# Where tiles begin in SBUF: small tiles first, matmul operands at multiples of 512 bytes

## The chip, the core and the metric

The kernel runs on one NeuronCore of a Trainium2 chip as one launch. The metric is the device time of that launch in microseconds, the median of three runs. Besides it there is one profiled execution, from which all rows below are taken; its span runs from the first to the last instruction of the program and doesn't contain what lies around them.

## What is computed

A trunk of two layers over 256 tokens of width 1024, everything in float32:

```python
for i in range(DEPTH):                       # DEPTH = 2
    y = gmlp_mixer(x, ...) if i == 0 else mlstm_mixer(x, ...)
    x = layer_norm(ALPHA * x + y, ln1_g[i], ln1_b[i])
    x = layer_norm(ALPHA * x + swiglu(x, ffn_w_gate[i], ffn_w_up[i], ffn_w_down[i]),
                   ln2_g[i], ln2_b[i])
    gate = jax.nn.sigmoid(x @ ple_w_gate[i] + ple_b_gate[i])
    x = x + gate * (p[i] @ ple_w_proj[i])
```

The gMLP mixer is two products of width 3072 with a gating over positions between them. The mLSTM mixer is an input product, a short convolution, block-diagonal q, k and v, a causal matrix of 256 x 256 for each of four heads, and an output product. SwiGLU has 2816 hidden features.

## The kernel before

Every weight is read once, as blocks of 128 x 1024 float32 (512 KB), loaded ahead by the SP queue into slots named `raw`. ScalarE and VectorE split each block into two float32r parts, high and low, whose sum is the block (`split`, L136); they lie side by side in one tile `w` of 8192 bytes for each partition. Activations are split in the same way. Each product is made of three matmuls, high*high, high*low and low*high.

There are two kinds of products. In `mm_feat` (L195 to L197) a piece of 128 x 128 of the weight block is the stationary operand and 256 tokens of x (`xh`, `xl`) are the moving one. In `mm_tok` (L190 to L192) and `mm_part` (L216 to L219) 128 tokens (of `xh` and `xl`, or of the hidden features `h`) are the stationary operand, and 512 columns of the weight block move. Every matmul has a weight load of its own: 5367 of each.

The order of the work is that of the program text. TensorE goes through gMLP (`vps`, then `ups`, `svps` and the first `acc`), SwiGLU of layer 0 (`first`, `pg` and `pu`, `acc`), the embedding's gate (`gate`), mLSTM (`zf`, `xmps`, `zps`, `qps`, `gates`, `s`, `num`, `acc`) and SwiGLU and gate of layer 1. Transposes are called `tp`.

All tiles of SBUF come from one pool `sb`. A tile without a tag keeps its place for the whole program. A tile with a tag goes through a number of slots of the size of the largest tile of the tag (`BUFS`, L126). Places are given out in the order in which the text first asks for a tile or a tag, each rounded up to 32 bytes. At the bottom of every partition the program reserves a scratch area in which descriptors of dynamic DMAs would be generated, 16384 bytes by default; four constants follow in 128 bytes, then the pool.

With the sizes added up in that order, the tiles that matmuls read begin in the kernel before at these places, given as the remainder of the byte address by 512:

| tiles | remainder |
|---|---|
| `xh`, `xl`, `xn`, and all slots of `s`, `m2`, `raw` and `w` | 160 |
| slots of `b8` (the weight blocks in `WIDE`, `ws`, `vn`, `bdm`, `pt`, ...) and of `row` (`xm`) | 448 |
| slots of `h` (hidden features, `q`, some `xm`, `phi`, `plo`) | 224 |
| `ident`, `ones_r` | 128 |
| `wx` | 256 |

`xh` and `xl` are at 160 because `ident` (512 bytes) and `mhalf` (8 bytes, in 32) lie ahead of them behind 16384 + 128 bytes. Pieces of a tile that a matmul reads begin at multiples of 512 bytes from the tile's start, those of `wx` at multiples of 64. The last tile ends 224 bytes below the top of the partition.

Of the kernel before, what the change touches and what calls it, by code (L numbers as in the profile page):

```python
# [14 lines left out]
P = 128  # L15
D = 1024
S = 256
# [27 lines left out]
# Weight blocks that are kept while token tile 1 is still in a norm; they have  # L45
# slots of their own, and some are loaded earlier than their place in the order of use.
# [6 lines left out]
def down_blocks(f):  # L53
    """the feature blocks that go down after block f is made"""
    return range(4) if f == 3 + LAG else [f - LAG] if f > 3 + LAG else []


def weight_plan(a):
    """The weight blocks in the order in which they are used."""
    plan = []  # L60

    def add(key, ap):
        plan.append((key, ap))

    for c in range(6):
        for kp in range(4):
            add(("v", c, kp), a["gm_v"][c, kp])
    add(("u", 0), a["gm_u"][0])
    add(("u", 1), a["gm_u"][1])
    for s in range(NU + LAG_S):  # L70
        if s + 2 < NU:
            add(("u", s + 2), a["gm_u"][s + 2])
        if s >= LAG_S:
            add(("wo", s - LAG_S), a["gm_wo"][s - LAG_S])

    def ffn(l):
        add(("pj", l, 0), a["ple_proj"][l, 0])
        for n in ("g", "u"):
            for kp in range(4):
                add((n, l, kp), a["ffn_" + n][l, kp])  # L80
        for f in range(4, NF + LAG):
            for n in ("g", "u") if f < NF else ():
                add((n, l, f), a["ffn_" + n][l, f])
            for e in down_blocks(f):
                add(("d", l, e), a["ffn_d"][l, e])
        add(("pj", l, 1), a["ple_proj"][l, 1])
        for k in range(KD):
            add(("pg", l, k), a["ple_gate"][l, k])

    ffn(0)  # L90
    for kp in range(4):
        add(("z", kp), a["ml_z"][kp])
    for s in range(NI + 2):
        if s < NI:
            add(("xm", s), a["ml_xm"][s])
        if s >= 2 and s % 4 == 2:
            add(("bdv", s // 4), a["ml_bdv"][s // 4])
        if s in Z_AFTER_XM:
            add(("z", Z_AFTER_XM[s]), a["ml_z"][Z_AFTER_XM[s]])
    for f in range(8, NI):  # L100
        add(("z", f), a["ml_z"][f])
    for f in range(NI):
        add(("mo", f), a["ml_wo"][f])
    ffn(1)
    by_key = dict(plan)
    moved = set(EARLY.values())
    order = []
    for key, _ in plan:
        if key not in moved:
            order.append(key)  # L110
        if key in EARLY:
            order.append(EARLY[key])
    return [(key, by_key[key]) for key in order]
# [3 lines left out]
def trunk(ctx, tc, a, out):  # L117
# [7 lines left out]
    # Slots of SBUF by size, shared by all phases.  # L125
# [8 lines left out]
    def split(hi, lo, src, fast=False, sub=dve):  # L134
        """float32r parts whose sum is src"""
        return dve.tensor_copy(hi, src) if fast else act.copy(hi, src), sub.tensor_tensor(lo, src, hi.bitcast(F32), ALU.subtract)  # L136

    # ---- weights: blocks [128, n <= 1024], loaded ahead and split (index 0
    # the high parts, index 1 the low) ----
# [4 lines left out]
    def issue_after(ops):  # L144
        """what is emitted in this context comes behind ops on their engines"""
        stack = ExitStack()
        for op in ops:
            stack.enter_context(tc.issue_after(op.ins))
        return stack
# [32 lines left out]
    ident = sb.tile([P, P], F32, name="ident")  # L182
    mhalf = sb.tile([P, 2], F32, name="mhalf")
# [15 lines left out]
    def feat_from_x(ps, w):  # L199
        """ps[128 features, 256 tokens] = (x w)^T"""  # L200
        for k in range(KD):
            mm_feat(ps, w, slice(k * P, (k + 1) * P), xh[:, k, :], xl[:, k, :], k == 0, k == KD - 1)

    def tok_from_x(ps, t, ws, before=(None, None)):
        """ps[128 tokens of tile t, 512] = x w; ws: 4 blocks of two k each.
        before: a step of the low part and what to emit before it"""
        for i in range(2):
            for k in range(KD):
                if i == 1 and k == before[0]:
                    before[1]()  # L210
                mm_part(ps, i, t, k, ws[k // 2], HALF[k % 2])

    def mm_part(ps, i, t, k, w, c):
        """the products with the high (i = 0) or low part of x"""
        if i == 0:
            pe.matmul(ps, xh[:, k, TOK[t]], w[:, 0, c], start=k == 0, stop=False)  # L216
            pe.matmul(ps, xh[:, k, TOK[t]], w[:, 1, c], start=False, stop=False)
        else:
            pe.matmul(ps, xl[:, k, TOK[t]], w[:, 0, c], start=False, stop=k == KD - 1)  # L219

    class Down:
        """y[tok, 1024] summed over n blocks of features; token tile 1 of the
        last HOLD blocks comes after all of token tile 0."""
# [58 lines left out]
    # ================= layer 0: gated MLP over positions =================  # L282
# [23 lines left out]
    vst = sb.tile([P, 2, 6, 6], F32, name="vst")  # L306
    vs = []
    for c in range(6):
        if c == 4:
# [8 lines left out]
            gmp = sb.tile([P, NU, 2], F32, name="gmp")  # L318
            sp.dma_start(gmp, a["gm_gb"])
            ones_r = sb.tile([P, P], F32R, name="ones_r")  # L320
            ones = sb.tile([P, 2], F32, name="ones")
            cmask = sb.tile([P, P], F32, name="cmask")
# [3 lines left out]
            # R[g, t] = sum_s ws[g, t, s], the same in all partitions  # L326
# [24 lines left out]
    vmv = sb.tile([P, 2, 2], F32, name="vmv")  # L351
    vrs = sb.tile([P, 2], F32, name="vrs")
# [7 lines left out]
    def norm_v(c, t):  # L360
        """(v - mean) / deviation; the gain and the offset come with sv"""
        if t == 0:
            vns[c] = tl("b8", [P, 2, 2, 512], F32R, "vn")
        v, o = vns[c], vs[c][:, t, :]
        dve.tensor_scalar(o, o, vmv[:, t, 0:1], vrs[:, t:t + 1], ALU.subtract, ALU.mult)
        split(v[:, 0, t, :], v[:, 1, t, :], o)
# [10 lines left out]
    def sv_block(f):  # L377
# [6 lines left out]
        # gain (ws n) + (offset R + b_s)  # L384
# [20 lines left out]
    def load_p(l):  # L405
        """p^T in parts, kept over the channel mixer"""
        pr = tl("m2", [P, 2, S], name="pr")
        sp.dma_start(pr, a["pT"][l])
        pts[l] = tl("b8", [P, 2, 2, S], F32R, "pt")
        split(pts[l][:, 0], pts[l][:, 1], pr)  # L410
# [16 lines left out]
    # ================= SwiGLU, norms, per-layer embedding =================  # L427
    def channel_mixer(l, acc, last, hook=None):
# [20 lines left out]
        # The first 512 features by token tile, so that token tile 0 runs  # L449
        # while token tile 1 is still in the norm.  # L450
# [96 lines left out]
    # ================= layer 1: mLSTM =================  # L547
    selIF = sb.tile([16, 2, 4], F32, name="selIF")
    wx = sb.tile([P, 2 * NI, 16], F32R, name="wx")
    par = sb.tile([P, NI, 7], F32, name="par")  # L550
    gbias = sb.tile([4, 2], F32, name="gbias")
    bmask = sb.tile([P, 32, 4], F32, name="bmask")
    wm = sb.tile([P, 2, NI, 4], F32R, name="wm")

    def mlstm_prepare():
# [18 lines left out]
        def products(terms, width):  # L574
            """sum of c[tile, b] g[tile, :, b] over b and the terms"""
# [14 lines left out]
        # S = q k^T = xc (Wq Wk^T) xc^T, so that k need not be made  # L590
        s = products([(0, load("wk4", a["ml_wk4"], 4))], 4)
        split(wm[:, 0], wm[:, 1], s)
        # The gates' weights carried through the blocks of q, k and v:
        # gates = xm (Wv Gv) + xc (Wq Gq + Wk Gk)
# [4 lines left out]
    def mlstm(embed1):  # L599
# [15 lines left out]
        # the block diagonals Wq Wk^T of 8 blocks of 128 channels each  # L615
# [86 lines left out]
        def s_block(f):  # L702
            """S^T[s, t] = q_t . k_s for s <= t in blocks of 128"""
# [29 lines left out]
        # ---- gates: a = i - B, G_t = max(0, max_{s<=t} a_s), B = cumsum(log f);  # L733
        # P^T[s, t] = S^T * scale * exp(a_s - G_t) ----
# [7 lines left out]
        cols = sb.tile([P, 4, 4], F32, name="cols")  # L742
        ph = []
        gs = tl("s", [16, S], name="gs")
        with tc.manual_schedule(engines={mybir.EngineType.Activation}):
# [23 lines left out]
            # exp(-m), kept finite  # L769
# [26 lines left out]
        def pv_block(h):  # L796
# [15 lines left out]
            # h = num / max(|den|, exp(-m)), then its norm over the head  # L812
# [56 lines left out]
def lay_out(inputs):  # L869
    """Rearranges the inputs so that each block of weights is one transfer  # L870
    with 4 KB in a row for each partition."""
# [4 lines left out]
    def feat(w):  # L876
        """[1024, n*128] -> [n, 128 (k in block), 8 (block of k) * 128]"""
        return w.reshape(KD, P, -1, P).transpose(2, 1, 0, 3).reshape(-1, P, D)

    def tok(w):  # L880
        """[1024, n*512] -> [n, 4 (pairs of blocks of k), 128, 2 * 512]"""
        return w.reshape(4, 2, P, -1, 512).transpose(3, 0, 2, 1, 4).reshape(-1, 4, P, D)

    def mixed(w):
        """the first 512 columns as tok, the others as feat"""
        return np.concatenate([tok(w[:, :512])[0], feat(w[:, 512:])])

    def diag(w):
        """[512, 4, 4] -> block diagonals [16, 128, 128]"""
# [6 lines left out]
    def part(w):  # L896
        """[2048, ...] -> [128, 16, ...]"""
# [26 lines left out]
    def over_block(w):  # L924
        """[512 blocks, 4 (b), n] -> [128, 16, n, 4 (b)], each block's rows for all its 4 channels"""
# [31 lines left out]
```

## Time and profile before

| | |
|---|---|
| median of three runs | 857.32 us (856.63 to 857.6) |
| span of the profiled execution | 855.1 us |
| TensorE busy | 846.4 us, 5367 matmuls |
| VectorE busy | 580.4 us |
| ScalarE busy | 452.7 us |
| granted TensorE clock | 0.999 of full over the span |
| moved by DMA | 155.62 MB, 182 GB/s |

Matmuls are pipelined, and the duration that the trace gives to one overlaps that of the next. What a matmul takes from the time of the kernel is therefore read as a spacing, the time from its start to the start of the next one. In the timeline this is the difference of two rows' first columns. In the chain of waits a run of equal matmuls stands in one row with its count, and time by count is the spacing.

### The profile page before, as it was taken

Reading aid. Unit: us, or ns where it says so; the run is one execution under the profiler, and the core shown is the slowest. Engines: PE = TensorE matmul, PEld = TensorE weight load, DVE = VectorE, ACT = ScalarE, POOL = GpSimd, SP = SyncE. Lnnn points to the kernel's source line nnn. Section 1 sums busy time; section 2 is a strip of 40 time slices with the busy share of each in tenths; the row PEclk is TensorE's granted clock in tenths of the full one; section 3 lists DMA queues with packets and bytes.
Section 4 is the critical chain, followed back from the end, with each engine's and each line's share of the span. In section 5 each row is a group of like instructions: output and inputs, shape, how many; then the busy total and the mean of one; then the engine's idle time right before and its main releaser. Section 6 shows DMA issues by size and latency. Waiting matters only on the chain.

```text
span 855.1 us, 13770 instructions
## 1 busy us (share of the span) xinstructions
PE 846.4 (99%) x5367; PEld 759.1 (89%) x5367; DVE 580.4 (68%) x831; ACT 452.7 (53%) x722; POOL 154.9 (18%) x197
## 2 busy tenths in 40 slices
PE   8999999999999999999999999999999999999997
PEld 5889999998888999999889999897888899999986
DVE  6667985667854546466878877689884545476574
ACT  6565655455444444365347777777643444455422
POOL 1021653443100001500102333133310000000010
PEclk9999999999999999999999999999999999999999
DMA  8885465557375555568234444263655655577501
GB/s 294 287 300 169 149 212 180 171 203 243 140 247 181 194 176 192 178 229 279 82 111 161 136 136 144 73 222 124 239 162 184 197 176 195 176 243 249 194 2 50
DMA packets 44714, 155.62 MB, mean 182 GB/s; under 512 B 5224, under 2 KB 5992, under 8 KB 44648
## 3 DMA queue, kind: packets, MB, share of 16 engines
q1 hardware_dynamic: 44360, 154.47, 53.7%
q8 instruction: 42, 0.69, 0.3%
q10 hardware_dynamic: 288, 0.26, 0.1%
q14 instruction: 24, 0.20, 0.1%
HBM read 153.67 MB, written 1.05 MB: 181 GB/s over the span
## 4 chain that ended last, share of the span: by engine, by line
PE 93%; DVE 3%; DMA 1%; ACT 1%; POOL 0%; issue 0%; SPq 0%; DVEq 0%; ACTq 0%; POOLq 0%
PE acc L190 9%; PE acc L192 9%; PE acc L191 9%; PE pu L196 4%; PE pu L195 4%; PE pu L197 4%; PE pg L197 4%; PE pg L195 4%; PE pg L196 4%; PE ups L197 3%; PE ups L195 3%; PE ups L196 3%; PE vps L192 2%; PE vps L191 2%; PE vps L190 2%; PE xmps L195 2%
## 5 line engine op out<-in xcount | busy, mean ns | idle before, releaser
L136 DVE TENSOR_TENSOR w<-raw,w 128x1024 fp32r<-128x1024 f32 (+1 forms) x277 | 334.5, 1219 | 169.3 <-ACT w L136 168.0
L136 ACT CAST w<-raw 128x1024 fp32r<-128x1024 f32 (+1 forms) x276 | 284.9, 1040 | 199.2 <-issue 57.0
L190 PE MATMUL acc<-w,h 128*128 128x512 f32 x336 | 133.5, 397 | 0.8 <-ACT hn L830 0.8
L191 PE MATMUL acc<-w,h 128*128 128x512 f32 x336 | 132.8, 395 | 0.3 <-DVE h L136 0.3
L192 PE MATMUL acc<-w,h 128*128 128x512 f32 x336 | 132.8, 395 | 0.0
L195 PE MATMUL pu<-xh,w 128*128 128x256 f32 x288 | 81.5, 283 | 0.0
L196 PE MATMUL pu<-xl,w 128*128 128x256 f32 x288 | 81.5, 283 | 0.0
L195 PE MATMUL pg<-xh,w 128*128 128x256 f32 x288 | 81.5, 283 | 0.0
L197 PE MATMUL pu<-xh,w 128*128 128x256 f32 x288 | 81.4, 283 | 0.0
L197 PE MATMUL pg<-xh,w 128*128 128x256 f32 x288 | 81.3, 282 | 0.0
L196 PE MATMUL pg<-xl,w 128*128 128x256 f32 x288 | 81.1, 282 | 0.0
L192 PEld LDWEIGHTS acc<-w,h 128*128 128x128 f32 x336 | 63.2, 188 | 15.5
L190 PEld LDWEIGHTS acc<-w,h 128*128 128x128 f32 x336 | 63.4, 189 | 13.9 <-ACT hn L830 1.3
L191 PEld LDWEIGHTS acc<-w,h 128*128 128x128 f32 x336 | 63.2, 188 | 13.0 <-DVE h L136 0.7
L248 POOL TENSOR_SCALAR ve<-mv 128x1 f32<-128x1 f32 x8 | 6.2, 776 | 276.8 <-DVE mv L268 276.8
L196 PEld LDWEIGHTS pg<-xl,w 128*128 128x128 f32 x288 | 54.9, 191 | 1.5
L195 PEld LDWEIGHTS pg<-xh,w 128*128 128x128 f32 x288 | 54.9, 191 | 1.4
L195 PEld LDWEIGHTS pu<-xh,w 128*128 128x128 f32 x288 | 55.3, 192 | 0.0
L196 PEld LDWEIGHTS pu<-xl,w 128*128 128x128 f32 x288 | 55.3, 192 | 0.0
L197 PEld LDWEIGHTS pu<-xh,w 128*128 128x128 f32 x288 | 55.3, 192 | 0.0
L197 PEld LDWEIGHTS pg<-xh,w 128*128 128x128 f32 x288 | 54.9, 191 | 0.0
L197 PE MATMUL ups<-xh,w 128*128 128x256 f32 x192 | 54.2, 282 | 0.0
(237 smaller groups left out, 1803.3 us busy)
## 6 DMA issues: line engine op xcount, KB each, us to landing
raw<-in_ffn_g SPq DMA_DIRECT2D x44, 512.0 KB, 3.5
raw<-in_ffn_u SPq DMA_DIRECT2D x44, 512.0 KB, 3.5
raw<-in_ffn_d SPq DMA_DIRECT2D x44, 512.0 KB, 3.6
raw<-in_gm_u SPq DMA_DIRECT2D x24, 512.0 KB, 3.5
raw<-in_gm_wo SPq DMA_DIRECT2D x24, 512.0 KB, 3.5
raw<-in_gm_v SPq DMA_DIRECT2D x23, 512.0 KB, 5.5
raw<-in_ple_gate SPq DMA_DIRECT2D x16, 512.0 KB, 4.5
raw<-in_ml_z SPq DMA_DIRECT2D x16, 512.0 KB, 3.5
```

Of the source, the lines that this page charges most:

```text
L136: return dve.tensor_copy(hi, src) if fast else act.copy(hi, src), sub.tensor_tensor(lo, src, hi.bitcast(F32), ALU.subtract)
L190: pe.matmul(ps, lh, w[:, 0, c], start=start, stop=False)
L191: pe.matmul(ps, ll, w[:, 0, c], start=False, stop=False)
L192: pe.matmul(ps, lh, w[:, 1, c], start=False, stop=stop)
L195: pe.matmul(ps, w[:, 0, c], h, start=start, stop=False)
L196: pe.matmul(ps, w[:, 0, c], l, start=False, stop=False)
L197: pe.matmul(ps, w[:, 1, c], h, start=False, stop=stop)
L248: pool.tensor_scalar(ve[:, :n], var, EPS, None, ALU.add)
```

## The change

The tiles that are smaller than 512 bytes, or read by no matmul, are asked for first, and then the tiles of 512 bytes and more. Of the small ones `mhalf`, `ones`, `vmv`, `vrs`, `gmp`, `selIF` and `gbias` take 32 + 32 + 32 + 32 + 192 + 32 + 32 = 384 bytes. `vst` is asked for as 512 bytes, of which 288 are used as before; `par` (448) and `cols` (64) make 512 together. The reserved scratch goes from 16384 to 8192 bytes. No instruction is added or taken away, and no shape or order of the work is changed. The other lines of the diff take out comments.

```diff
+    mhalf = sb.tile([P, 2], F32, name="mhalf")
+    ones = sb.tile([P, 2], F32, name="ones")
+    vmv = sb.tile([P, 2, 2], F32, name="vmv")
+    vrs = sb.tile([P, 2], F32, name="vrs")
+    gmp = sb.tile([P, NU, 2], F32, name="gmp")
+    selIF = sb.tile([16, 2, 4], F32, name="selIF")
+    gbias = sb.tile([4, 2], F32, name="gbias")
     ident = sb.tile([P, P], F32, name="ident")
-    mhalf = sb.tile([P, 2], F32, name="mhalf")
+    ones_r = sb.tile([P, P], F32R, name="ones_r")
+    cmask = sb.tile([P, P], F32, name="cmask")
+    bmask = sb.tile([P, 32, 4], F32, name="bmask")
+    wm = sb.tile([P, 2, NI, 4], F32R, name="wm")
+    par = sb.tile([P, NI, 7], F32, name="par")
+    cols = sb.tile([P, 4, 4], F32, name="cols")
+    vst = sb.tile([P, P], F32, name="vst")[:, :72].rearrange("p (t c n) -> p t c n", t=2, c=6)
+    wx = sb.tile([P, 2 * NI, 16], F32R, name="wx")
     xh = sb.tile([P, KD, S], F32R, name="xh")
     xl = sb.tile([P, KD, S], F32R, name="xl")
...
-    vst = sb.tile([P, 2, 6, 6], F32, name="vst")
...
-            gmp = sb.tile([P, NU, 2], F32, name="gmp")
...
-            ones_r = sb.tile([P, P], F32R, name="ones_r")
-            ones = sb.tile([P, 2], F32, name="ones")
-            cmask = sb.tile([P, P], F32, name="cmask")
...
-    vmv = sb.tile([P, 2, 2], F32, name="vmv")
-    vrs = sb.tile([P, 2], F32, name="vrs")
...
-    selIF = sb.tile([16, 2, 4], F32, name="selIF")
-    wx = sb.tile([P, 2 * NI, 16], F32R, name="wx")
-    par = sb.tile([P, NI, 7], F32, name="par")
-    gbias = sb.tile([4, 2], F32, name="gbias")
-    bmask = sb.tile([P, 32, 4], F32, name="bmask")
-    wm = sb.tile([P, 2, NI, 4], F32R, name="wm")
...
-        cols = sb.tile([P, 4, 4], F32, name="cols")
...
-    nc = _bacc.Bacc("TRN2", target_bir_lowering=False, num_devices=1)
+    nc = _bacc.Bacc("TRN2", target_bir_lowering=False, num_devices=1, dynamic_dma_scratch_size=8192)
```

## Rows read from the trace of the kernel before

**Rows 1.** The page: busy time, share of the span, instructions of each engine.

```profile
PE 846.4 (99%) x5367; PEld 759.1 (89%) x5367; DVE 580.4 (68%) x831; ACT 452.7 (53%) x722; POOL 154.9 (18%) x197
```

**Rows 2.** The page: clock granted to TensorE, tenths, in 40 slices; the chain by engine.

```profile
PEclk9999999999999999999999999999999999999999
...
PE 93%; DVE 3%; DMA 1%; ACT 1%; POOL 0%; issue 0%; SPq 0%; DVEq 0%; ACTq 0%; POOLq 0%
```

**Rows 3.** Timeline, TensorE, SwiGLU of layer 0: start us, duration us, line, operands.

```profile
400.23 0.28 PE L195 MATMUL pg<-xh,w 128*128 128x256 f32 x1
...
403.35 0.28 PE L197 MATMUL pu<-xh,w 128*128 128x256 f32 x1
403.47 0.40 PE L190 MATMUL acc<-w,h 128*128 128x512 f32 x1
...
411.88 0.39 PE L190 MATMUL acc<-w,h 128*128 128x512 f32 x1
```

**Rows 4.** Timeline, TensorE, the first product of gMLP.

```profile
20.32 0.39 PE L190 MATMUL vps<-w,xh 128*128 128x512 f32 x1
...
23.72 0.39 PE L190 MATMUL vps<-w,xh 128*128 128x512 f32 x1
```

**Rows 5.** Chain of waits, several stretches: start us, us, line, matmuls in the run.

```profile
82.43 0.47 PE svps L383 x4
...
222.14 0.87 PE tp L256 x8
...
228.16 1.86 PE first L219 x8
...
451.19 1.81 PE zf L219 x8
...
497.19 0.24 PE gates L687 x2
```

**Rows 6.** Timeline, TensorE: the first matmuls of 256 columns behind a run of 512.

```profile
305.20 0.28 PE L195 MATMUL pg<-xh,w 128*128 128x256 f32 x1
305.31 0.27 PE L196 MATMUL pg<-xl,w 128*128 128x256 f32 x1
...
306.13 0.28 PE L197 MATMUL pg<-xh,w 128*128 128x256 f32 x1
```

**Rows 7.** TensorE's groups by line and form: count, busy us, mean ns, idle before.

```profile
L190 PE MATMUL acc<-w,h 128*128 128x512 f32 x336 | 133.5, 397 | 0.8 <-ACT hn L830 0.8
...
L195 PE MATMUL pu<-xh,w 128*128 128x256 f32 x288 | 81.5, 283 | 0.0
...
L197 PE MATMUL ups<-xh,w 128*128 128x256 f32 x192 | 54.2, 282 | 0.0
...
L190 PE MATMUL vps<-w,xh 128*128 128x512 f32 x96 | 37.6, 392 | 1.8 <-ACT w L136 1.0 <-DVE w L136 0.7
...
L195 PE MATMUL xmps<-xh,w 128*128 128x256 f32 x128 | 36.7, 287 | 0.0
...
L195 PE MATMUL zps<-xh,w 128*128 128x256 f32 x96 | 28.0, 292 | 0.0
...
L216 PE MATMUL first<-w,xh 128*128 128x512 f32 x64 | 25.3, 396 | 0.0
...
L216 PE MATMUL gate<-w,xh 128*128 128x512 f32 x56 | 22.2, 396 | 0.0
...
L383 PE MATMUL svps<-ws,vn 128*128 128x256 f32 x96 | 15.1, 280 | 0.0
```

**Rows 8.** Busy time by stretch (PE, PEld, DVE, ACT, POOL; clock, DMA share, GB/s).

```profile
260.00:400.00 140.00, 140.00 (x962) 129.88 (x962) 78.11 (x90) 66.31 (x89) 16.00 (x29) 1.00 0.60 203
...
455.00:540.00 85.00, 85.00 (x720) 83.63 (x718) 71.17 (x136) 61.19 (x143) 30.46 (x31) 1.00 0.44 146
```

**Rows 9.** The page: GB/s in 40 slices of the span; DMA queues, packets, MB, share.

```profile
GB/s 294 287 300 169 149 212 180 171 203 243 140 247 181 194 176 192 178 229 279 82 111 161 136 136 144 73 222 124 239 162 184 197 176 195 176 243 249 194 2 50
...
q1 hardware_dynamic: 44360, 154.47, 53.7%
...
q10 hardware_dynamic: 288, 0.26, 0.1%
```

## The prediction, made before the result was known

> **What bounds the kernel now.** I read the page's busy times first: TensorE is busy 846.4 of 855.1 us, VectorE 580.4 [rows 1]. The chain of waits says the same, 93% of it is TensorE [rows 2], and the clock granted is the full level, 2.4 GHz, in every slice [rows 2]. So the time is a number of matmuls by the spacing of their starts, and the next thing to read is the timeline, where the spacing stands. In SwiGLU 26 steps of 256-column matmuls take 403.35 - 400.23 = 3.12 us, 120.0 ns each, and 36 steps of 512-column ones take 8.41 us, 233.6 ns each [rows 3]. In gMLP's first product 15 steps of 512 columns take 3.40 us, 226.7 ns each [rows 4]. Same shape, same engine, no wait in either, and 7 ns apart: that is what has to be explained.
>
> The operands' places do differ. In `vps`, and in `zf` with 1.81/8 = 226 ns [rows 5], both operands begin at remainder 160. In `acc` the stationary operand is at 224 and the moving one at 160; in `first`, with 1.86/8 = 232.5 ns [rows 5], the moving one is at 448 and the stationary one at 160. So unequal remainders go with some 6 to 7 ns more for each matmul of 512 columns. For 256 columns it is the other way round and weaker: equal remainders (160 and 160) settle at 120.0, after eight matmuls at 0.93/8 = 116 ns behind a run of `acc` [rows 6]; `svps` and `gates` take 0.47/4 and 0.24/2, some 118 and 120 ns [rows 5].
>
> A second reading matters more. Between 256 and 512 columns at equal remainders lie 226.7 - 120.0 = 106.7 ns for 256 columns, one clock of 2.4 GHz for each. What is left over is the same for both shapes: 13.3 ns for each matmul, whatever its length. A fixed price for each instruction looks like one at its ends, which is where a start inside a line of memory would show: 13.3 ns is what 128 bytes of the moving row take at 2.4 GHz, and no remainder in the table (160, 224, 448) is a multiple of 128. No row shows a large operand that begins at such a multiple, so the trace can't say what happens there.
>
> **The change part by part.** *The places.* 8192 + 128 bytes are at remainder 128, the seven small tiles add 384, so `ident` begins at a multiple of 512; everything behind it is a multiple of 512 long (`par` with `cols`, `vst`, the eight slots of `c` together), so each tile named in the table comes to remainder 0. Exceptions are `selIF`, `ones` and the pieces of `wx`, which few and short matmuls read. *The scratch.* All bulk transfers are on hardware queues, q1 and q10 [rows 9], and POOL issues none; halving it costs nothing, and if a reserve were missed it would show as slower landings, which up to now are hidden. *Instructions.* None is added, removed or moved; no wait is added.
>
> What has to be priced is the spacing. The counts [rows 7]: 512 columns, `acc` 3 x 336 = 1008, `first` and `gate` 3 x (64 + 56) = 360, `vps` and `zf` 3 x 96 + 48 = 336, and `num` and `pps` 84; 256 columns, `pg`, `pu`, `ups`, `xmps` and `zps` 3 x (2 x 288 + 192 + 128 + 96) = 2976, and 368 small ones of which `svps` is 96. By the spacings above (119.6 for the 2976, as a third of those in some runs go at 116; 117.5 for the 368; 233 for the 84) that is 235.5 + 83.7 + 76.2 + 19.6 + 355.9 + 43.2 = 814 of the 855 us. The rest is the start, the transposes and waits, and I leave it as it is.
>
> Lower bound of the price of an aligned pair: nothing of the 13.3 ns goes, only the inequality. Upper bound: all of it goes. For 256 columns the weight loads then set the spacing, one for each matmul; `tp`, whose matmuls of 128 columns are shorter than a load, shows 0.87/8 = 108.75 ns [rows 5], 2.1 above 106.7. I give 512 columns the same 2.1, so 215.4.
>
> All of it gone: 1008 x 18.2 + 360 x 17.1 + 336 x 11.3 + 84 x 17.6 = 29.8 us for the long ones, 2976 x 10.85 + 368 x 8.75 = 35.5 us for the short ones, 65 us together. Half of it gone (220.0 and 113.3): 21.6 + 20.2 = 42 us. I take a value between them, 53.5 us, because the load's stream and the moving one still run at the same time and the small step in `acc` shows that they meet. Of this I give back 3.5 us to waits. The covers are there: in SwiGLU VectorE works 78 of 140 us, and DMA moves 203 GB/s [rows 8], which would have to be 217, while it did 294 to 300 in the first slices [rows 9]; the tightest stretch is mLSTM's input with VectorE at 71 of 85 us [rows 8], where 5 us less on TensorE would still leave 9. So 50 us, and as the span of the profiled execution lies 2.2 us below the median, the sum is put on the median: 857.3 - 50 = 807.
>
> The Trainium skill's page "TensorE: Matmul & The Clock Gate", section "Back-to-back issue gap", gives N / 2.4 + 2.5 ns for a warm matmul, 109.2 and 215.8 here; the rows show 120.0 and 226.7 or more, so the rule isn't met in the kernel before, and an estimate by its figures would be about the upper bound, 65 us.
>
> **The rivals.** *Only equality counts.* The 13.3 ns belong to the pair of streams or to float32r and stay; the change makes all remainders equal, which for 512 columns has been seen at 226.7 and for 256 at 120. Gain 1008 x 6.9 + 360 x 5.8 + 84 x 6.3 = 9.6 us, loss 2976 x 0.4 + 368 x 2.5 = 2.1 us: 849.8. For it: it uses nothing but spacings that the rows show; and `svps`, with both operands at 448, is at 118 [rows 5], near the 120 of an equal pair at 160, so another place for the pair changed little. Against: 448 and 160 are both off a multiple of 128, so this tests nothing beyond 64 bytes.
>
> *Addresses don't matter.* What sets `acc` apart from `vps` is something else, and the time stays 857.3. Against: `zf` and `first` differ in nothing but the place of the moving block, and stand 6 ns apart [rows 5]. The Trainium skill's page "SBUF — State Buffer", section "Door 1: The DMA port swizzle", speaks for this one: it knows lines of 16 bytes and full speed for reads that run along them, and all remainders here are multiples of 16. By that rule the spacing of `first` and `zf` would be equal; the trace doesn't agree.
>
> *Slower.* At equal remainders the spacings seen are 9 and 17 times 13.3 ns, as if the two streams could only start in step. If `acc`, whose stationary tile has just been written by ScalarE and VectorE, doesn't find the step at 17, the next one is 18, 240 ns: 1008 x 6.4 + 360 x 7.5 + 84 x 7 = 9.8 us lost, and 2.1 us as above on the short ones, 869. It decides wherever an aligned pair needs more than 226.7 ns. For it: short matmuls at unequal remainders stand at 118 now, below 120 [rows 5]. Against: `zf` keeps 226 with freshly written operands.
>
> That the change doesn't do what it says is excluded by the sum of the sizes above, short of a tile that is placed in another order than the text asks for it.
>
> **How the numbers follow.** Places of multiples of 512 take away the fixed price, wholly or in part: 0.50, 792 to 822, value 807. Only equality counts: 0.27, 847 to 853. Addresses don't matter: 0.11, 856 to 859. Slower: 0.12, 859 to 872. The range from 795 to 859 leaves out the slower case and the lower edge of the first, some 0.17. About 0.2% is what a measurement of this kernel can tell from no change; faster by more than that are the first two cases, 0.77, the same 0.11, slower 0.12. Faster cases hold most of the chance, and the likeliest one's own range is 792 to 822.
>
> **What would show it.** In the timeline of the changed kernel: `pg` and `pu` at 109 to 113 ns a step and `acc` and `vps` at 215 to 220, alike among themselves, if the forecast is right. `pg` still at 120.0 and `acc` at 226.7 would mean that only equality counts; `acc` still at 233.6 and `vps` at 226.7, that places aren't the cause; `acc` at 240, the slower rival. The clock row, the counts and the durations of VectorE's splits should stay as they are. The forecast is wrong if the 13.3 ns are there with every operand at remainder 0, or if waits before `w` grow by more than the 3.5 us that I gave them.

## The result, and the profile after

The changed kernel takes 851.97 us (851.45 to 852.55), the kernel before, timed beside it, 857.46 us: a ratio of 0.994, 95% interval 0.9926 to 0.9954. That is 5.5 us less, where 50 had been forecast. It is faster by 0.6%, and the time lies near what the rival *Only equality counts* gave, 849.8.

The page of the changed kernel: busy time, share of the span and instructions by engine, the granted clock in 40 slices, the chain of waits by engine, and the costliest group of VectorE (count, busy us, mean ns).

```profile
PE 842.0 (99%) x5367; PEld 761.8 (90%) x5367; DVE 580.2 (68%) x831; ACT 452.9 (53%) x722; POOL 154.9 (18%) x197
...
PEclk9999999999999999999999999999999999999999
...
PE 95%; DVE 2%; DMA 1%; POOL 0%; ACT 0%; issue 0%; DVEq 0%; SPq 0%; ACTq 0%
...
L136 DVE TENSOR_TENSOR w<-raw,w 128x1024 fp32r<-128x1024 f32 (+1 forms) x277 | 334.5, 1219 | 168.0 <-ACT w L136 167.2
```

Against [rows 1, 2] the counts are the same, the clock is the full level in every slice, and VectorE works as long as before. TensorE still bounds the kernel. So the difference has to stand in the spacing of the matmuls, and the timeline of the changed kernel shows it (start us, duration us, line, operands), in SwiGLU of layer 0, the place of [rows 3].

```profile
398.92 0.28 PE L212 MATMUL pu<-xh,w 128*128 128x256 f32 x1
...
401.68 0.28 PE L214 MATMUL pu<-xh,w 128*128 128x256 f32 x1
401.80 0.40 PE L207 MATMUL acc<-w,h 128*128 128x512 f32 x1
...
402.96 0.39 PE L209 MATMUL acc<-w,h 128*128 128x512 f32 x1
...
404.54 0.39 PE L207 MATMUL acc<-w,h 128*128 128x512 f32 x1
```

The first two rows are 23 steps apart: 2.76 / 23 = 120.0 ns, what `pg` and `pu` took before, although both operands now begin at a multiple of 512. `acc` takes 1.16 / 5 = 232 ns in its first five steps and 1.58 / 7 = 226 in the next seven, where it was 233.6 throughout. The chain of the changed kernel (start us, us, matmuls in the run) shows two others:

```profile
82.78 0.48 PE svps L393 x4
...
227.73 1.82 PE first L236 x8
```

`first` went from 1.86 / 8 = 232.5 ns in [rows 5] to 1.82 / 8 = 227.5. `svps` went from 0.47 to 0.48; over all its runs of four the step has a mean of 116.4 ns before and 119.8 after, though its operands were equal before as well. Runs of four don't settle: what lies ahead of them counts, too.

All spacings of a trace can be added up by group. A step is the time from one start to the next. It counts as dense up to 245 ns (512 columns), 128 ns (256) or 118 ns (shorter); a longer one holds a wait, and what it has above the mean dense step of its row is counted with the waits. For the dense steps, count times mean gives:

| group | before: count x ns = us | after: count x ns = us |
|---|---|---|
| `pg`, `pu`, `ups`, `xmps`, `zps` | 2949 x 119.5 = 352.4 | 2949 x 119.8 = 353.3 |
| `acc` | 1002 x 233.4 = 233.8 | 1002 x 228.3 = 228.7 |
| `first`, `gate` | 354 x 232.7 = 82.4 | 352 x 227.3 = 80.0 |
| `vps`, `zf` | 328 x 227.2 = 74.5 | 325 x 226.8 = 73.7 |
| small ones | 63.4 | 63.8 |
| in steps with a wait, above a dense step | 11.9 | 13.5 |
| the rest: `num`, `pps`, the dense part of steps with a wait, start and end | 36.7 | 37.8 |
| span | 855.1 | 850.8 |

5.1 us came from `acc`, some 2 from `first` and `gate`. The 256-column matmuls gave back 0.9, the small ones 0.4, the waits 1.6. `vps` and `zf` gave next to nothing: three of their steps hold a wait now and have moved to the rows with waits, as have two of `first` and `gate`. In the two profiled executions the difference is 4.3 us, in the medians 5.5; the remaining 1.2 us isn't resolved by one profile of each.

### The profile page after: what moved, and what is told of

It is laid out like the page before. It is cut to its first block, busy times and chain, and to the rows that moved or that the text cites. A ratio compares the mean times of both kernels' runs of the same rounds, so it can differ in the third digit from the quotient of the medians.

```text
span 850.8 us, 13770 instructions
## 1 busy us (share of the span) xinstructions
PE 842.0 (99%) x5367; PEld 761.8 (90%) x5367; DVE 580.2 (68%) x831; ACT 452.9 (53%) x722; POOL 154.9 (18%) x197
## 4 chain that ended last, share of the span: by engine, by line
PE 95%; DVE 2%; DMA 1%; POOL 0%; ACT 0%; issue 0%; DVEq 0%; SPq 0%; ACTq 0%
PE acc L207 9%; PE acc L208 9%; PE acc L209 9%; PE pu L214 4%; PE pu L213 4%; PE pu L212 4%; PE pg L214 4%; PE pg L213 4%; PE pg L212 4%; PE ups L214 3%; PE ups L213 3%; PE vps L207 3%; PE ups L212 3%; PE vps L208 3%; PE vps L209 3%; PE xmps L212 2%
## 5 line engine op out<-in xcount | busy, mean ns | idle before, releaser
L207 PE MATMUL acc<-w,h 128*128 128x512 f32 x336 | 131.8, 392 | 0.9 <-ACT hn L833 0.9
L208 PE MATMUL acc<-w,h 128*128 128x512 f32 x336 | 131.5, 391 | 0.2 <-DVE h L136 0.2
L209 PE MATMUL acc<-w,h 128*128 128x512 f32 x336 | 130.7, 389 | 0.0
L209 PEld LDWEIGHTS acc<-w,h 128*128 128x128 f32 x336 | 63.1, 188 | 13.5
```

Of the source, the lines that this page charges most:

```text
L207: pe.matmul(ps, lh, w[:, 0, c], start=start, stop=False)
L208: pe.matmul(ps, ll, w[:, 0, c], start=False, stop=False)
L209: pe.matmul(ps, lh, w[:, 1, c], start=False, stop=stop)
```

## The experiments

Three questions: whether the place itself counts or only the difference of the two operands' places; which difference is best; and what the 13.3 ns are. "Difference" below is the stationary operand's remainder less the moving one's. In three of the kernels, the sweeps, TensorE does nothing but groups of 48 matmuls into one bank, each with its own load; they leave out the whole computation of the reference. Their "steady spacing" is the mean of the last 24 steps of a group. The first matmuls of each sweep's first group come at double the spacing, 213 ns at 256 columns and more at 512, so the equal pair of 256 columns is read from the finer sweep.

### A sweep over places, shapes and types

```diff
+    for i in range(N):          # N = 48
+        om = dm // size + (i % 8) * 512
+        os = ds // size + (i * 3 % 16) * 512 // size
+        pe.matmul(ps[:m, :n], w[:, os:os + m], x[:, om:om + n], start=i == 0, stop=i == N - 1)
```

`r64` in a name means that the moving operand begins at remainder 0 and the stationary one at 64, `a128` that both begin at remainder 128, `few` that the stationary operand has 16 columns in place of 128, `bf` that both are bf16.

> This kernel leaves out the whole computation. TensorE runs groups of 48 matmuls, each with a weight load of its own, with nothing to wait for; a group is one choice of columns (256 or 512), type, and bytes past a multiple of 512 of the moving and of the stationary operand. Groups r: moving at 0, stationary at r. Groups a: both at a. Groups few: 16 columns of weights only. Groups bf: bf16. If only equality counts: all groups a at 226.7 and 120.0 ns a matmul, r0 the same, other r at 229 to 236 (512) and 113 to 118 (256). If there is a fixed price for each matmul that depends on where lines of 128 bytes begin: a128 and r0 lower than a32, a64 and a160, near 215 and 109. If the weight load's stream is what costs: the groups few at 215 and 109, with any place, and the groups bf at 216 and 109.

The timeline of the sweep by group: start us, time to the last end, operands, count.

```profile
51.76 5.91 PE L57 MATMUL n256r256x<-mov,sta 128*128 128x256 f32 x48
57.51 5.82 PE L57 MATMUL n256r320x<-mov,sta 128*128 128x256 f32 x48
...
86.02 5.91 PE L57 MATMUL n256a128x<-mov,sta 128*128 128x256 f32 x48
91.77 5.91 PE L57 MATMUL n256a160x<-mov,sta 128*128 128x256 f32 x48
...
108.72 5.61 PE L57 MATMUL n256few160x<-mov,sta 128*16 128x256 f32 x48
114.17 5.41 PE L57 MATMUL n256bf0x<-movb,stab 128*128 128x256 bf16 x48
119.42 5.40 PE L57 MATMUL n256bf64x<-movb,stab 128*128 128x256 bf16 x48
...
146.77 11.36 PE L57 MATMUL n512r64x<-mov,sta 128*128 128x512 f32 x48
157.97 11.40 PE L57 MATMUL n512r96x<-mov,sta 128*128 128x512 f32 x48
...
180.37 11.16 PE L57 MATMUL n512r192x<-mov,sta 128*128 128x512 f32 x48
191.36 11.06 PE L57 MATMUL n512r256x<-mov,sta 128*128 128x512 f32 x48
202.26 11.36 PE L57 MATMUL n512r320x<-mov,sta 128*128 128x512 f32 x48
...
257.42 11.09 PE L57 MATMUL n512a128x<-mov,sta 128*128 128x512 f32 x48
268.35 11.08 PE L57 MATMUL n512a160x<-mov,sta 128*128 128x512 f32 x48
...
301.29 11.25 PE L57 MATMUL n512few160x<-mov,sta 128*16 128x512 f32 x48
312.38 10.53 PE L57 MATMUL n512bf0x<-movb,stab 128*128 128x512 bf16 x48
322.75 10.52 PE L57 MATMUL n512bf64x<-movb,stab 128*128 128x512 bf16 x48
```

From start to start, over 48: with 64 bytes of difference a group of 512 columns takes 11.20 us, 233 ns a matmul; with 192, 10.99 us, 229; with 256, 10.90 us, 227; and with both at 128, where the forecast expected a drop, 10.93 us, 228, no less than at 256. At 256 columns the group with both at 128 takes 5.75 us, 119.8 ns a matmul. In bf16 it is 10.37 us, 216, at 512 columns. The steady spacings, with a few of the finer sweep below:

| pair | 256 columns, ns | 512 columns, ns |
|---|---|---|
| difference 0 (finer sweep) or 256 | 120.0 | 226.7 |
| both moved, to 32, 64, 128, 160 or 448 | 120.0 | 226.7 |
| difference 64 or 320 | 117.8 (113.3 in the finer sweep) | 233.3 |
| difference 128 or 384 | 118.8 and 118.7 | 232.7 (128: 233.3 in the finer sweep) |
| difference 192 or 448 | 117.8 (192: 113.3 in the finer sweep) | 228.9 |
| loads of 16 columns, both at 0 / at 160 | 113.3 / 113.3 | 231.7 / 231.1 |
| bf16, difference 0 or 64 | 109.2 | 215.8 |

At the places tried the place of a pair doesn't count; the difference does, and 256 is as good as none. The two lengths want different things: the equal pair is the best for 512 columns and the worst of this table for 256. And the 13.3 ns of an equal pair stay at every place; bf16 leaves 2.5 of them at either difference. The Trainium skill's page "TensorE: Matmul & The Clock Gate", section "Back-to-back issue gap", gives N / 2.4 + 2.5 ns as the gap of an isolated matmul. The bf16 groups, each matmul with a load of its own, agree with it to a tenth of a nanosecond (109.2 and 215.8), the float32r ones lie 4 to 19 ns above it.

The load is felt in float32r, and not as a simple price: 16 columns of load in place of 128 give 113.3 instead of 120.0 at 256 columns, and 231 to 232 instead of 226.7 at 512. The same page of the Trainium skill, section "Step-by-step: what each phase is for", says that loading the next weights doesn't take read bandwidth from the running matmul. The float32r groups show that load and matmul aren't independent, but no run here shows whether read bandwidth is the reason.

### The changed kernel with everything 160 bytes higher

```diff
+    sb.tile([P, 40], F32, name="pad")
     ident = sb.tile([P, P], F32, name="ident")
```

> The changed kernel with 160 bytes of padding ahead of ident: every operand is at remainder 160 by 512 instead of 0, all equal. If only equality counts: 852 us as the changed kernel, acc 226.7 and pg 120.0 ns. If the multiples of 512 count: acc and vps apart from the changed kernel's, 855 to 857 us.

851.94 us (851.1 to 852.06), ratio 0.994 (0.9925 to 0.9955): the changed kernel's time with no large operand at a multiple of 512. Its timeline, 25 steps:

```profile
382.74 0.28 PE L214 MATMUL pg<-xl,w 128*128 128x256 f32 x1
...
385.74 0.28 PE L215 MATMUL pu<-xh,w 128*128 128x256 f32 x1
```

3.00 / 25 = 120.0 ns; `acc` has the mean of the changed kernel, 228.3. What the change does, it does by making remainders equal, and the multiple of 512 has no part in it.

### The changed kernel with `h` alone moved by 64 bytes

The slots of `h` begin 64 bytes higher, so that `acc` gets its old difference back, 224 - 160 = 64.

```diff
         cf = tl("cf", [P, P], name="cf")
+        if f == 0:
+            sb.tile([P, 16], F32, name="padh")
```

> The changed kernel with 64 bytes of padding ahead of the slots of h alone: the stationary operand of acc is at remainder 64, its moving one at 0. If equality counts: acc from 227 to some 233 ns, 1008 times 6 = 6 us of the gain lost, 857 to 858 us, while first, gate and vps stay at 226.7. If places don't matter for acc: 852 us.

855.27 us (854.84 to 856.91), ratio 0.998 (0.9971 to 0.9989). In the timeline `acc` is back at its old spacing, 11 steps in 2.57 us, 233.6 ns:

```profile
387.65 0.40 PE L207 MATMUL acc<-w,h 128*128 128x512 f32 x1
...
390.22 0.40 PE L209 MATMUL acc<-w,h 128*128 128x512 f32 x1
```

`first` stays at 227.3. The sum by groups gives +5.4 us for `acc` and -1.0 for the 256-column ones, whose first matmuls behind such an `acc` are closer, as in [rows 6]; the spans differ by 4.4 and the medians by 3.3. That is less than the 5 to 6 us that were expected to be lost, in part because of these closer ones. Still, most of the change's gain is this one difference.

### The scratch alone

```diff
-    nc = _bacc.Bacc("TRN2", target_bir_lowering=False, num_devices=1)
+    nc = _bacc.Bacc("TRN2", target_bir_lowering=False, num_devices=1, dynamic_dma_scratch_size=8192)
```

> The kernel before with the reserved scratch halved and nothing else: every tile lies 8192 bytes lower, all remainders as before. If only remainders count: 857 us, acc at 233.4 and vps at 227 ns. If the smaller scratch does something: another time, and other landings of the DMAs.

857.38 us against 857.01, ratio 1.0003 (0.9994 to 1.0013). All tiles move down by 8192 bytes, no remainder changes, and `acc` is as in the kernel before, 2.57 / 11 = 233.6 ns:

```profile
388.03 0.40 PE L190 MATMUL acc<-w,h 128*128 128x512 f32 x1
...
390.60 0.40 PE L192 MATMUL acc<-w,h 128*128 128x512 f32 x1
```

### `xh` and `xl` moved against the weights by 64 bytes

By the sweep the 2976 matmuls of 256 columns would rather have unequal operands. Here `xh` and `xl` begin at 64, and all else at 0. As the moving operand of 256 columns they make a difference of -64, which is 192 modulo 256; as the stationary one of 512 columns, 64.

```diff
+    sb.tile([P, 16], F32, name="padx")
     xh = sb.tile([P, KD, S], F32R, name="xh")
     xl = sb.tile([P, KD, S], F32R, name="xl")
+    sb.tile([P, 112], F32, name="pady")
```

> The changed kernel with xh and xl 64 bytes past a multiple of 512, all others at 0: the moving operand of pg, pu, ups, xmps and zps (2976 matmuls of 256 columns) and the stationary one of vps, zf, first and gate (696 of 512) differ from their partners. If equality costs the short ones: their spacing goes from 120 to 116 to 118, 6 to 12 us gained, and 696 times 6.3 = 4.4 us lost on the long ones, together 844 to 850 us. If the 120 ns are the weight load's own pace: no gain, 856 us.

849.97 us (849.72 to 850.31), ratio 0.992 (0.9904 to 0.9937). The timeline of SwiGLU and one run of `first` in the chain:

```profile
383.08 0.28 PE L214 MATMUL pu<-xh,w 128*128 128x256 f32 x1
...
385.79 0.28 PE L216 MATMUL pu<-xh,w 128*128 128x256 f32 x1
```

```profile
228.60 1.87 PE first L238 x8
```

`pu` is at 2.71 / 23 = 117.8 ns and `first` at 1.87 / 8 = 233.8: both as the sweep has them. The 256-column group gives 353.3 - 346.5 = 6.8 us, `first`, `gate`, `vps` and `zf`, which read `xh` as the stationary operand, take some 4 of it back. The time is at the upper end of the 844 to 850 that were expected.

### A finer sweep, in steps of 16 bytes

It is the sweep above with differences of 0, 16, ... 240, and with loads of 32 and 64 columns.

> This kernel leaves out the whole computation, as the first sweep did. Groups r: float32r, moving operand at a multiple of 512 bytes, 128 columns of weights r bytes past one, r in steps of 16 up to 240. If the two streams meet in banks of 64 bytes with a period of 256 bytes: r0 at 120.0 and 226.7, r64, r192 near 117.8, r128 near 118.6, and the steps of 16 between them lie between. If only whole lines of 64 bytes mattered: r16, r32 and r48 as r0 or as r64. Groups m: 32 or 64 columns of weights instead of 128: if the load's stream costs by its length, they lie between 113.3 (16 columns) and 117.8 to 120 (128 columns).

```profile
61.34 5.61 PE L54 MATMUL n256r64x<-mov,sta 128*128 128x256 f32 x48
66.78 5.86 PE L54 MATMUL n256r80x<-mov,sta 128*128 128x256 f32 x48
```

The group with a difference of 64 takes 5.44 us here, 113.3 ns each, and took 117.8 in the first sweep, with the same operands at the same places. So there is more than one steady spacing, and the difference alone doesn't choose it. 192 also has 113.3 in this run. For 512 columns the equal pair is the best (16 and 240 are as good, 226.7 here, but 16 had 233.3 in the sweep below), then 192 with 228.9; the others have 230 to 234.4. That makes 192 the place to try, for both lengths.

Two of the expectations failed. The steps of 16 bytes don't lie in order between their neighbours: at 256 columns 144, 160 and 240 have 120.0, as the equal pair. And the loads don't cost by their length: with 16, 32, 64 and 128 columns the equal pair has 113.3, 117.8, 113.3 and 120.0 ns at 256 columns, and 231.7, 231.7, 230.0 and 226.7 at 512.

### `xh` and `xl` at 192

```diff
+    sb.tile([P, 48], F32, name="padx")
     xh = sb.tile([P, KD, S], F32R, name="xh")
     xl = sb.tile([P, KD, S], F32R, name="xl")
+    sb.tile([P, 80], F32, name="pady")
```

> The changed kernel with xh and xl 192 bytes past a multiple of 512 instead of 0. The sweep gives 117.8 ns for 256 columns with the stationary operand 64 bytes ahead by 256 (-192), as for 192, and 229.0 ns for 512 columns with it at 192, where 64 gave 233.4. So the 2976 short ones gain 2.3 ns as in the run with 64 bytes, and the 696 long ones lose 2.3 instead of 6.6: 3 us less than that run's 849.97, so 847 us. If the sweep doesn't carry over to the kernel: 850 us or more.

844.65 us (843.71 to 845.29), ratio 0.985 (0.9834 to 0.9867). Two places in its timeline:

```profile
254.95 0.28 PE L214 MATMUL pu<-xh,w 128*128 128x256 f32 x1
...
257.56 0.28 PE L216 MATMUL pu<-xh,w 128*128 128x256 f32 x1
...
392.81 0.28 PE L214 MATMUL pg<-xh,w 128*128 128x256 f32 x1
...
398.46 0.39 PE L209 MATMUL acc<-w,h 128*128 128x512 f32 x1
```

The same work stands at 2.61 / 23 = 113.5 ns in one run and at 5.65 / 48 = 117.7 in another. The trace has 120 runs of 20 and more matmuls of 256 columns; from their ninth matmul on, 28 of them have 113 ns and 92 have 118, and none anything between. Mean of the group 116.9, `first` and `vps` 229. The 847 us expected had all of them at 117.8; at 116.9 the group is 2.7 us shorter, about what the time lies below it.

### The weights of `b8` at 192 too

```diff
+            if c == 0:
+                sb.tile([P, 48], F32, name="padb")
             v2 = tl("b8", [P, 2, 2, 512], name="v")
+            if c == 0:
+                sb.tile([P, 80], F32, name="padd")
```

On top of `xh` and `xl` at 192, this makes the operands of `first` and `gate` equal again, but for a quarter of their matmuls: the last two blocks of the up projection in `first` and of the eight in `gate` aren't in `WIDE` (L47) and lie in `w`, at 0.

> As the run before, and the slots of b8 at 192 too, so that first and most of gate have equal operands again: some 270 matmuls from 229 to 226.7, 0.6 us; against it num (36) goes to 233 and pps (48) to 229, 0.3 us. 846.5 to 847 us, hardly apart from the run before. If equality counted for more than these few matmuls: 845 us or less.

844.83 us (844.44 to 845.46), ratio 0.9855 (0.9841 to 0.987), no difference to the kernel without it. `first` and `gate` have 229.6 ns, not the 227.3 of the changed kernel. The timeline shows why:

```profile
237.14 0.39 PE L236 MATMUL first<-w,xh 128*128 128x512 f32 x1
...
242.81 0.40 PE L235 MATMUL first<-w,xh 128*128 128x512 f32 x1
...
244.66 2.02 PE L238 MATMUL first<-w,xl 128*128 128x512 f32 x8
```

On the blocks of `b8` the equal pair does settle: 25 steps take 5.67 us, 226.8 ns each. The next 8, on the two blocks in `w`, have the difference 192 again and take 1.85 us, 231 ns each. Each time the difference changes some steps go by before the spacing settles, so the mean stays above both.

### What chooses the pattern: the group ahead?

The group of 256 columns with a difference of 64, behind groups of eleven lengths and places, and the equal pair behind three.

> This kernel leaves out the whole computation. The same group (256 columns, stationary operand 64 bytes past the moving one's place by 512) follows groups of other kinds. If the two streams fall into one of several steady patterns, and the phase at entry picks it: some of these groups at 117.8 and some at 113.3 ns, the same lead giving the same value again; the groups with equal places (r0) at 120.0 behind any lead. If the two values of the two sweeps had another cause (a position in time, the bank of PSUM): no order by lead.

```profile
27.85 5.82 PE L60 MATMUL athen256r64x<-mov,sta 128*128 128x256 f32 x48
33.51 11.16 PE L60 MATMUL blead512r192x<-mov,sta 128*128 128x512 f32 x48
...
123.58 5.60 PE L60 MATMUL hthen256r64x<-mov,sta 128*128 128x256 f32 x48
129.02 11.07 PE L60 MATMUL ilead512r0x<-mov,sta 128*128 128x512 f32 x48
```

Behind ten of the eleven it takes 5.66 / 48 = 117.9 ns, and behind one, 256 columns with a difference of 192, 5.44 / 48 = 113.3. One case of eleven fits that what runs ahead chooses, but doesn't show it, and the sweep gives no rule: 256 columns at 48 ran ahead of the 113.3 in the finer sweep, and here 117.8 stands behind them twice. The equal pair has a mean of 120.0 behind all three.

### `h` moved as well, by 256 and by 192 bytes

```diff
         cf = tl("cf", [P, P], name="cf")
+        if f == 0:
+            sb.tile([P, 64], F32, name="padh")
```

This stands on top of `xh` and `xl` at 192; in a second kernel the tile has 48 elements in place of 64.

> The run with xh and xl at 192, and h 256 bytes past a multiple of 512. If the period is 256 bytes: acc at 226.7 ns as with h at 0, and the time the same, 844.7 us within 1. If it takes multiples of 512: acc at 229 to 234 ns, 2 to 7 us lost.

> The run with xh and xl at 192, and h at 192 too. acc has its stationary operand 192 ahead: 229.0 ns by the sweep, 1008 times 1.6 to 2.3 = 2 us lost, 847 us, if the short matmuls behind it keep their spacings. If the phase at entry picks the pattern of the short ones: their share at 113.3 instead of 117.8 changes although their own operands lie where they lay; each 10% more of the 2976 at 113.3 is worth 1.3 us.

With 256: 844.08 us (843.66 to 844.24), ratio 0.9848 (0.9831 to 0.9864); `acc` at 227.4 and the same 28 of 120 runs at 113 ns as with `xh` and `xl` moved alone. 256 bytes are no difference, in the kernel too.

With 192: **837.9 us** (837.24 to 839.07), ratio 0.9777 (0.9762 to 0.9791), the best of all. Its page's busy row, and its timeline:

```profile
PE 828.1 (99%) x5367; PEld 744.7 (89%) x5367; DVE 580.2 (69%) x831; ACT 452.3 (54%) x722; POOL 154.8 (19%) x197
```

```profile
392.15 0.28 PE L214 MATMUL pu<-xh,w 128*128 128x256 f32 x1
...
394.87 0.39 PE L209 MATMUL acc<-w,h 128*128 128x512 f32 x1
...
397.16 0.39 PE L210 MATMUL acc<-w,h 128*128 128x512 f32 x1
```

24 steps of `pu` in 2.72 us are 113.3 ns, and 10 of `acc` in 2.29 us are 229. `acc` is slower than with an equal pair (mean 229.2 against 227.4), but 113 of the 120 runs of 256 columns now have 113 ns: 336.3 us for the group, 8.3 less than before `h` was moved. These runs don't read `h`; `acc`, which runs ahead of them, does. The traces show it run by run. All 50 runs right behind `acc` (32 of `pg`, 18 of `ups`) have 118 ns with `h` at 0 or 256, and all 50 have 113 with `h` at 192; each of the 36 `pu` runs has the spacing of the `pg` run ahead of it; and with `h` at 0 and at 256 all 120 runs agree one by one. Here the work ahead of a run chose its pattern.

### All four at 192

`xh`, `xl`, `h` and `b8`, the two edits above together.

> xh, xl, h and the slots of b8 at 192, raw, w, row and ident at 0: as the run with xh, xl and h at 192, and first and most of gate have equal operands. By their own places 0.6 us less than its 837.9 us; if the phase at entry picks the pattern of the short ones, their share at 113.3 stays near what it was there, since h and w, which run ahead of them, lie as there: 837 to 838 us.

839.64 us (838.99 to 839.83), ratio 0.9795 (0.9779 to 0.9812). It is above the kernel without `b8`, and above the 837 to 838 expected; `acc` has 230.2 ns, and `vps` and `zf` have 230.3, though their places are as without `b8`. `first` has 1.82 / 8 = 227.5 in runs whose blocks are all in `b8`, and 1.85 / 8 = 231 where half of them are in `w`:

```profile
226.85 1.82 PE first L238 x8
...
233.23 1.85 PE first L238 x8
```

### All kernels together

Means of dense steps, and how the 120 runs of 20 and more matmuls of 256 columns divide by their spacing from the ninth on.

| kernel | median us | 256 columns, ns | runs at 113 / 118 / 120 | `acc`, ns | `first`, `gate`, ns |
|---|---|---|---|---|---|
| before (beside the changed one) | 857.46 | 119.5 | 0 / 0 / 120 | 233.4 | 232.7 |
| scratch alone | 857.38 | 119.5 | 0 / 0 / 120 | 233.4 | 232.7 |
| changed | 851.97 | 119.8 | 0 / 0 / 120 | 228.3 | 227.3 |
| all at 160 | 851.94 | 119.8 | 0 / 0 / 120 | 228.3 | 227.4 |
| `h` at 64 | 855.27 | 119.5 | 0 / 0 / 120 | 233.6 | 227.3 |
| `xh`, `xl` at 64 | 849.97 | 117.5 | 9 / 111 / 0 | 228.5 | 233.3 |
| `xh`, `xl` at 192 | 844.65 | 116.9 | 28 / 92 / 0 | 227.4 | 229.1 |
| the same, `b8` at 192 | 844.83 | 116.9 | 25 / 95 / 0 | 227.7 | 229.6 |
| `xh`, `xl` at 192, `h` at 256 | 844.08 | 116.9 | 28 / 92 / 0 | 227.4 | 229.1 |
| `xh`, `xl` at 192, `h` at 192 | 837.9 | 114.1 | 113 / 7 / 0 | 229.2 | 229.1 |
| all at 192 | 839.64 | 114.3 | 109 / 11 / 0 | 230.2 | 229.5 |

## Why the prediction was right or wrong

*What bounds the kernel.* Right: every microsecond that moved, moved in the spacing of matmuls or in waits, at the same clock and the same counts.

*Unequal remainders cost 6 to 7 ns at 512 columns; at 256 it is the other way round and weaker.* The first half is right: the sweep has 233.3 against 226.7 for the difference that `acc` had (64), and moving `h` alone by 64 bytes brought 233.6 back. In `first` the difference is 160 - 448, 224 modulo 256, where the finer sweep has 233.3, and three quarters of its matmuls have it. The other quarter, on the blocks in `w`, was equal already: in the trace of before the eight high steps on these blocks fall to 226 and 227 ns before the difference changes again. The second half has the sign right and is too weak: up to 6.7 ns, on three times as many matmuls. And the sign was luck: the short matmuls cited for it, `svps` and the first eight in [rows 6], have equal operands, so they show how a run starts and not what unequal remainders do.

*A fixed price of 13.3 ns goes, wholly or in part, when operands begin at multiples of 128 or 512.* This is the step that failed, and with it the 53.5 us. 106.7 + 13.3 and 213.3 + 13.3 were read as the ends of an instruction, where a start inside a line would show. But an equal pair has 120.0 and 226.7 ns at 0, 32, 64, 128, 160 and 448 alike, and the whole kernel takes the same time with everything at 160. The rows of before held equal pairs at two places, 160 and 448 [rows 3, 5], with 120 and 118 ns, little apart. That spoke for the rival, and the prediction set it aside since neither is a multiple of 128: an unseen case was given 0.50 on a numerical likeness. The upper bound had 256 columns at the 108.75 ns of `tp`; no float32r group of the sweeps settled below 113.3 there. The 13.3 ns go with the type: in bf16 2.5 are left. Whether that is because both streams have half the bytes isn't shown.

*Only equality counts.* The right rival, with 849.8 against 851.97. Its terms: `acc` was to give 7.0 us and gave 5.1, as it doesn't settle at once; in the changed kernel's timeline above five steps of each run behind `pu` are at 232 before 226.7 comes. `first` and `gate` were to give 2.1 and gave some 2. The loss on shorter matmuls was put at 2.1 and was 0.9 + 0.4. The 1.6 us of waits weren't in its sum.

*Addresses don't matter* is excluded by `h` at 64 and by 192. *Slower*: `acc` found the step at 226.7 with freshly written operands, so 240 ns didn't come; but that short matmuls at unequal remainders stand closer, which was said for it, was the more useful reading: taken further it leads to 837.9 us. The row cited there was the wrong one, `svps`, whose pair was equal; the sweep and the kernels with `xh` and `xl` moved carry it.

*The scratch costs nothing.* Right: 1.0003 (0.9994 to 1.0013).

*The waits.* 3.5 us were set aside against 50 us of gain; 1.6 came with a gain of 5.5. At 837.9 us they have grown by 2.9 over the kernel before (14.8 against 11.9), while its spacings gave 21.

What stays open: what chooses between the spacings that one pair of places can have (113.3 and 117.8 at 256 columns with a difference of 64, 226.7 and 233.3 at 512 with one of 16). The work ahead is part of it, as `h` at 192 shows. But no rule was found that gives the sweep as well: in the kernel 512 columns with a difference of 192 leave 113 behind them, in the last sweep 117.8. That the two streams meet in reading the same part of memory is a guess that fits a period of 256 bytes; no run shows it.

## What to carry to other kernels

Where matmuls with one load each bound a float32r kernel, read the spacing of their starts by group, and look at the difference of the two operands' places modulo 256, not at the places themselves: at 512 columns equal or 192 was best here, at 256 columns 64 or 192, and the best pair was found by padding one tile at a time. A row that doesn't exist in the trace is no ground for half the chance; a small sweep that puts one pair at several places gives the price directly. And the spacing of a run can depend on the run ahead, so the whole kernel has to be timed, not the group.

## What the runs showed of the hardware

- The spacing of float32r matmuls depends on the difference of the operands' start addresses, with a period of 256 bytes: 64 and 320, 128 and 384, 192 and 448 agree in pairs within 0.1 ns in the first sweep, and `h` at 256 left the kernel as it was with `h` at 0.
- The dependence turns round with the length: 120.0 for an equal pair against 113.3 to 119.8 for most others at 256 columns (120.0 also at 144, 160 and 240), 226.7 against 229 to 234.5 for most others at 512 (226.7 also at 240, and once at 16).
- A run doesn't start at its steady spacing: `acc` with equal operands takes five steps of 232 ns behind `pu` before 226.7 comes.
- There are several steady spacings for the same operands at the same places: 113.3 and 117.8 ns within one kernel. With `xh` and `xl` at 192 the place of `h`, which only the work ahead reads, moved all 50 runs behind `acc` from one to the other.
- A load of 16 columns instead of 128 makes matmuls of 256 columns closer (113.3) and those of 512 wider (231.1 and 231.7), both without a change of place; 32 and 64 columns don't lie in order between.
- bf16 showed none of this at the two differences tried: 109.2 and 215.8 ns at 0 and at 64.
